# A two-layer decoder step on one core: how the low parts of the second layer's weights are made

## The chip, the core and the metric

The kernel runs on one core of a Trainium2 chip. A core has five engines that run side by side and wait for each other by semaphores: TensorE (PE: matrix products, with PEld, its weight loads), VectorE (DVE), ScalarE (ACT), GpSimd (POOL), and SyncE (SP), which here only issues transfers. Sixteen DMA engines move data between the large memory (HBM), on-chip memory (SBUF), and within SBUF. Products land in PSUM, which DVE and ACT read. The metric is the device time of one execution in microseconds (us); lower is better. The kernel before took 1169.92 us, the median of three runs (1169.79 to 1174.06).

## What is computed

One inference step of a two-layer trunk, for a prompt of 512 tokens and 8 samples of 8 tokens (576 columns in all), width 1024, in float32. Layer one is a gated linear recurrence; then one shared key/value projection; layer two is sliding-window attention with queries and gates of its own:

```python
for layer in range(DEPTH):
    if layer < N_A_LAYERS:
        hp, sp = hgrn2_layer(hp, s_zero, w_in_a[layer], w_out_a[layer], norm_a[layer], onorm_a[layer], lb[layer])
        ...
        kv_p = shared_kv(hp, norm_kv, w_kv)
        kv_s = shared_kv(hs, norm_kv, w_kv)
    else:
        q, gate = swa_in(hp, w_in_b[j], norm_b[j])
        hp = swa_out(hp, swa_prompt(q, kv_p, sinks_b[j]), gate, w_out_b[j])
        q, gate = swa_in(hs, w_in_b[j], norm_b[j])
        hs = swa_out(hs, swa_sample(q, kv_s, cache_kv_window, sinks_b[j]), gate, w_out_b[j])
```

`swa_in` is an RMS norm and a product with `w_in_b` (1024 x 4096: queries and gates); `swa_out` multiplies the attention output by silu(gate) and by `w_out_b` (2048 x 1024) and adds the input.

## The kernel before

**Split products.** A product of float32 data is made of three products in a faster format: activations and weights are each split into a high part, rounded to that format, and a low part, the rest. PE adds high x high, high weight x low activation, and low weight x high activation. `product_cols` (L207) orders them so: eight matmuls (one for each 128 rows) with the high weights `whi` and the high activations, eight with `whi` and the low activations, and last eight with the low weights `wlo`. A weight tile is used for two halves of the columns, 48 matmuls in all.

**Weight tiles.** `split_weights` (L195) makes one tile of 128 x 1024. SP loads 512 KB from HBM into `raw` (three buffers in rotation); ACT casts it to `whi` (L200); `wlo` is raw minus high (L204). `whi` and `wlo` have two buffers each, so a cast for a tile waits until PE has finished with the tile before the last. A number called the share says how many eighths of the subtraction DVE does; POOL does the rest. It is 8 in layer one, 2 for the key/value weights, and `LO_B` = 0 in the second layer (L1406): there POOL makes every low part.

**The second layer's tiles.** 16 tiles of query weights (`bq`), 16 of gate weights (`bg`) and 16 of output weights (`o`). Fourteen of the last kind use `whi_o` and `wlo_o`; the two tiles of the closing product (`out_last`, L477) use the memory of the activations' own parts `xhi` and `xlo`, which are no longer needed by then. All splits go through `split_weights`.

**Order.** The attention of the second layer and the products with weight tiles are woven by a list written by hand (`ORDER`, `merged`), so that PE has products to do while scores, exponentials and turns of the attention run on DVE, ACT and POOL. A scheduler then lays out the instructions for each engine in order of priority; each engine works through its list strictly in that order and waits at the first instruction that is not ready. POOL's list in this layer holds the subtractions, half of the scalings of the probabilities P (L1136), the last step of the gates (`silu`, L1343, after three ACT passes over `lb`, L1340 to L1342) and copies of V (`Vd`, L1356).

**Names in the rows.** At the start of the layer, `u_norm_b`, `xhi`, `xlo` are the normalized activations (`scaled`, L515), `kf` (L1030) the scaled key/value products, and `pvw` (L1062) turns of `kf` on PE. `pbq`, `pbg`, `po`, `pz` are the products with query, gate, output and closing tiles. `QS` (L1286, L1289) and `Qs` (L1294) are the queries, high and low parts; `ohb`, `olb` (L1394, L1395, L1266, L1267) the two parts of the gated attention output; `hT` (L1334) the residual stream; `Ps`, `oS`, `sts` belong to the samples' attention; `P`, `ph`, `pk`, `low` to the prompt's.

The closing lines of the split:

```python
act.copy(hi[:, :n], raw[:, :n])
c = n * share[0] // 8
for eng, r in ((dve, slice(0, c)), (pool, slice(c, n))):
    if r.start < r.stop:
        eng.tensor_tensor(lo[:, r], raw[:, r], hi[:, r].bitcast(F32), ALU.subtract)
```

## Time and profile before

| | |
|---|---|
| time, median of three runs | 1169.92 us |
| the profiled execution, its own time | 1169.39 us |
| its span, first to last instruction | 1167.6 us |
| TensorE clock granted, mean of the span | 0.982 of full speed |
| DMA packets' share of the 16 engines, main queue | 28.0% |
| HBM read / written | 84.06 MB / 14.16 MB |

A row of the timeline gives the start and the duration in us, then engine, line, operation, what it writes and reads (output<-inputs, by the program's names), the shape, and how many like it were merged; in brackets stands the engine's idle time before it and what ended that. A row of the waits gives who waited for whom, the total in us, how often, and the longest. A row of groups gives the busy time in us and the mean in ns, then the idle time before and who ended it. A row that begins with two times and a colon is a stretch of the span: its length, then the busy time of PE, PE's weight loads, DVE, ACT and POOL with their instructions, the granted clock, the DMA share, and GB/s. Busy times of PE are modelled for pipelined matmuls, so a busy PE need not be at its peak.

### The profile page before, as it was taken

Reading aid. Unit: us, or ns where it says so; the run is one execution under the profiler, and the core shown is the slowest. Engines: PE = TensorE matmul, PEld = TensorE weight load, DVE = VectorE, ACT = ScalarE, POOL = GpSimd, SP = SyncE. Lnnn points to the kernel's source line nnn. Section 1 sums busy time; section 2 is a strip of 40 time slices with the busy share of each in tenths; the row PEclk is TensorE's granted clock in tenths of the full one; section 3 lists DMA queues with packets and bytes.
Section 4 is the critical chain, followed back from the end, with each engine's and each line's share of the span. In section 5 each row is a group of like instructions: output and inputs, shape, how many; then the busy total and the mean of one; then the engine's idle time right before and its main releaser. Section 6 shows DMA issues by size and latency. Waiting matters only on the chain.

```text
span 1167.6 us, 27339 instructions
## 1 busy us (share of the span) xinstructions
PE 1111.7 (95%) x10937; PEld 1078.1 (92%) x10937; DVE 895.4 (77%) x2090; ACT 702.1 (60%) x1700; POOL 340.7 (29%) x311
## 2 busy tenths in 40 slices
PE   5999999999999999999999987999999999999997
PEld 5999999999999999999999987989989999999986
DVE  8898776489984597893897779567787778777686
ACT  6776764466662567772767455557655764765545
POOL 1122221112121131110122155444543453454430
PEclk8999999999999999999999998989999999999999
DMA  5332233232332523332232332211212213112102
GB/s 154 100 112 86 84 109 112 59 110 76 110 117 66 147 74 113 97 107 74 76 111 77 103 91 74 68 55 56 73 39 71 74 55 91 56 55 73 56 19 82
DMA packets 161097, 98.01 MB, mean 84 GB/s; under 512 B 3897, under 2 KB 157546, under 8 KB 160938
## 3 DMA queue, kind: packets, MB, share of 16 engines
q1 hardware_dynamic: 160970, 96.26, 28.0%
q8 instruction: 86, 1.41, 0.5%
q14 instruction: 41, 0.34, 0.1%
HBM read 84.06 MB, written 14.16 MB: 84 GB/s over the span
## 4 chain that ended last, share of the span: by engine, by line
PE 45%; DVE 11%; ACT 6%; issue 2%; POOL 1%; DVEq 0%; ACTq 0%; POOLq 0%
PE pbg L211 7%; PE po L211 7%; PE pbq L211 5%; PE po L228 4%; PE pg L228 3%; PE pf L228 3%; PE pi L228 3%; PE pq L228 2%; PE pkv L211 2%; PE sc L1098 2%; ACT P L1127 1%; PE pav L1181 1%; PE pz L211 1%; DVE QS L1289 1%; PE pa L797 1%
## 5 line engine op out<-in xcount | busy, mean ns | idle before, releaser
L606 POOL TENSOR_TENSOR Xl<-Xl 128x72 f32<-128x72 f32 x80 | 50.3, 659 | 205.9 <-DVE Xl L603 204.7
L638 POOL TENSOR_TENSOR sg<-sg,lg 128x576 f32<-128x576 f32 x16 | 26.3, 1642 | 278.4 <-ACT lg L571 278.4
L200 ACT CAST whi_a<-raw_a 128x1024 fp32r<-128x1024 f32 x64 | 67.1, 1049 | 63.4 <-PE po L228 30.8
L204 DVE TENSOR_TENSOR wlo_a<-raw_a,whi_a 128x1024 fp32r<-128x1024 f32 x64 | 81.8, 1282 | 25.0 <-issue 23.6
L1127 ACT ACTIVATE P<-P,st 128x192 f32<-128x192 f32 (+2 forms) x128 | 54.1, 424 | 68.4 <-DVE st L1122 68.4
L1136 POOL TENSOR_SCALAR P<-P,st 128x192 f32<-128x192 f32 (+1 forms) x64 | 48.6, 769 | 117.9 <-DVE st L1129 99.4
L438 DVE TENSOR_TENSOR hT<-hT,po 128x576 f32<-128x576 f32 x32 | 24.1, 754 | 49.6 <-PE po L228 49.3
L200 ACT CAST whi_o<-raw_o 128x1024 fp32r<-128x1024 f32 x30 | 31.4, 1047 | 30.8 <-PE po L228 25.6
L204 POOL TENSOR_TENSOR wlo_bg<-raw_bg,whi_bg 128x1024 fp32r<-128x1024 f32 x16 | 38.4, 2402 | 35.5 <-ACT whi_bg L200 30.0
L228 PE MATMUL po<-oh,whi_o 128*128 128x288 f32 x256 | 42.8, 302 | 4.4 <-ACT whi_o L200 1.9
L211 PE MATMUL po<-olb,whi_o 128*128 128x288 f32 x224 | 43.0, 306 | 3.8 <-DVE olb L1395 1.9
L211 PE MATMUL po<-ohb,whi_o 128*128 128x288 f32 x224 | 43.6, 311 | 2.4 <-DVE Qs L1294 1.7
L662 POOL TENSOR_TENSOR vb<-vst,bmask 128x512 fp32r<-128x512 f32 x32 | 36.7, 1168 | 26.7 <-DVE vst L658 13.8
L204 POOL TENSOR_TENSOR wlo_bq<-raw_bq,whi_bq 128x1024 fp32r<-128x1024 f32 x16 | 38.8, 2430 | 19.2 <-ACT whi_bq L200 19.1
L228 PEld LDWEIGHTS po<-oh,whi_o 128*128 128x128 f32 x256 | 35.9, 188 | 6.3 <-ACT whi_o L200 2.2
L211 PE MATMUL pbq<-xhi,whi_bq 128*128 128x256 f32 (+1 forms) x256 | 41.4, 305 | 0.0
L211 PE MATMUL po<-ohb,wlo_o 128*128 128x288 f32 x224 | 41.3, 301 | 0.0
L228 PE MATMUL po<-ol,whi_o 128*128 128x288 f32 x256 | 40.5, 294 | 0.0
L211 PE MATMUL pbg<-xhi,whi_bg 128*128 128x288 f32 x256 | 40.5, 300 | 0.0
L228 PE MATMUL po<-oh,wlo_o 128*128 128x288 f32 x256 | 40.4, 294 | 0.0
L211 PE MATMUL pbg<-xhi,wlo_bg 128*128 128x288 f32 x256 | 40.1, 299 | 0.0
L204 POOL TENSOR_TENSOR wlo_o<-raw_o,whi_o 128x1024 fp32r<-128x1024 f32 x14 | 33.6, 2399 | 22.0 <-ACT whi_o L200 20.3
(385 smaller groups left out, 3761.4 us busy)
## 6 DMA issues: line engine op xcount, KB each, us to landing
raw_a<-in_w_in_a_dram SPq DMA_DIRECT2D x64, 512.0 KB
S<-in_state_hgrn_dram SPq DMA_DIRECT2D x32, 256.0 KB
out_dram<-S SPq DMA_DIRECT2D x32, 256.0 KB
raw_o<-in_w_out_a_dram SPq DMA_DIRECT2D x16, 512.0 KB
raw_bq<-in_w_in_b_dram SPq DMA_DIRECT2D x16, 512.0 KB
raw_bg<-in_w_in_b_dram SPq DMA_DIRECT2D x16, 512.0 KB
raw_o<-in_w_out_b_dram SPq DMA_DIRECT2D x16, 512.0 KB
xt<-in_x_prompt_dram SPq DMA_DIRECT2D x4, 512.0 KB
```

The source lines that it names most:

```text
L200: act.copy(hi[:, :n], raw[:, :n])
L204: eng.tensor_tensor(lo[:, r], raw[:, r], hi[:, r].bitcast(F32), ALU.subtract)
L211: pe.matmul(pm[:, : c1 - c0], w[:, k * width + w0 : k * width + w0 + P], x(k)[i][:, c0:c1], start=n == 0, stop=n == len(terms) - 1,)
L228: pe.matmul(pm[:, j, :HN], w[:, k * width + c0 : k * width + c0 + P], x(k, j), start=n == 0 and k == 0, stop=n == 2 and k == nk - 1,)
L438: dve.tensor_add(h2, h2, ps2(pm))
L606: pool.tensor_tensor(X8[:, :, j : j + 1], X8[:, :, j : j + 1], X8[:, :, k : k + 1], ALU.add)
L638: (pool if SGP else dve).tensor_tensor(sg, sg, l, ALU.mult)
L662: pool.tensor_tensor(t, view(vst.bitcast(F32), [[0, 4], [1, P]], off=half * P), view(bmask, [[1, 4], [0, P]]), ALU.mult,)
L797: pe.matmul(pa[32 * j : 32 * j + ns, c, t0 : t0 + nt], keys[:, c * P + s0 : c * P + s0 + ns], queries[:, c * P + t0 : c * P + t0 + nt], st ...
L1098: pe.matmul(sc[:, hf, k0[hf] :], QS[pr][:, 2 * n + hf, :], kk[:, g, ks], start=q == 0, stop=q == 1)
L1127: act.activation(x, x, AF.Exp, bias=st[:, a : a + 1], accum_out=st[:, 8 + a : 9 + a])
L1136: (pool if e == "p" else dve).tensor_scalar(x, x, st[:, 8 + a : 9 + a], None, ALU.mult)
```

## The change

In the second layer the low part is no longer a subtraction on POOL. ACT makes the high part as before; a second ACT instruction writes the negated high part into `wlo`; then a transfer that is issued from POOL's list, with addition, adds the raw tile to what stands in `wlo`, inside SBUF. The other splits (share 8 and share 2) are as they were.

```diff
-LO_B = 0
+LO_B = None
...
         hi, lo = parts or [wts.tile([P, 1024], F32R, tag=t, name=f"{t}_{name}") for t in ("whi", "wlo")]
+        if share[0] is None:
+            act.copy(hi[:, :n], raw[:, :n])
+            act.activation(lo[:, :n], hi[:, :n].bitcast(F32), AF.Copy, scale=-1.0)
+            pool.dma_start(lo[:, :n].bitcast(F32), raw[:, :n], accum_op=ALU.add)
+            return hi, lo
         act.copy(hi[:, :n], raw[:, :n])
```

The lines below L200 move down by five in the changed file. The instructions do not only change in kind; the scheduler also places some of them elsewhere. POOL's list at the start of the second layer, before:

```order
L521 TENSOR_TENSOR xlo<-u_norm_b_0_9540,xhi 128x288
L204 TENSOR_TENSOR wlo_bq_9715<-raw_bq_9712,whi_bq_9714 128x1024
L204 TENSOR_TENSOR wlo_bq_9781<-raw_bq_9778,whi_bq_9780 128x1024
L521 TENSOR_TENSOR xlo<-u_norm_b_1_9600,xhi 128x288
L521 TENSOR_TENSOR xlo<-u_norm_b_1_9608,xhi 128x288
L521 TENSOR_TENSOR xlo<-u_norm_b_1_9616,xhi 128x288
L521 TENSOR_TENSOR xlo<-u_norm_b_1_9624,xhi 128x288
L1356 CAST Vd_9704<-Vc 64x512 x4
```

The same place in POOL's list with the change:

```order
L526 TENSOR_TENSOR xlo<-u_norm_b_0_9540,xhi 128x288
L203 DMA wlo_bq_9715<-raw_bq_9712 128x1024
L526 TENSOR_TENSOR xlo<-u_norm_b_1_9600,xhi 128x288
L526 TENSOR_TENSOR xlo<-u_norm_b_1_9608,xhi 128x288
L526 TENSOR_TENSOR xlo<-u_norm_b_1_9616,xhi 128x288
L526 TENSOR_TENSOR xlo<-u_norm_b_1_9624,xhi 128x288
L203 DMA wlo_bq_9782<-raw_bq_9779 128x1024
L1361 CAST Vd_9704<-Vc 64x512 x4
```

Two subtractions in a row gave way to two transfers, the second of which stands behind all low parts of the normalized activations. ACT's list around the last query tile and the gate tile after it, before:

```order
L1341 ACTIVATE lb_13887<-lb_13887 128x512
L200 CAST whi_bq_14031<-raw_bq_14029 128x1024
L1342 ACTIVATE lb_13887<-lb_13887 128x512
L1286 CAST QS_0_13905<-pbq_0_13913 64x4x64 x2
L1127 ACTIVATE P_0_2_13942,st_0_2_13943<-P_0_2_13942,st_0_2_13943 128x192
L1124 ACTIVATE st_0_2_13943<-st_0_2_13943 128x4
L1127 ACTIVATE P_0_2_13942,st_0_2_13943<-P_0_2_13942,st_0_2_13943 128x192 x3
```

The same place in ACT's list with the change:

```order
L1347 ACTIVATE lb_13923<-lb_13923 128x512
L1291 CAST QS_0_13941<-pbq_0_13950 64x4x64 x2
L202 ACTIVATE wlo_bq_14069<-whi_bq_14068 128x1024
L1132 ACTIVATE P_0_2_13979,st_0_2_13980<-P_0_2_13979,st_0_2_13980 128x192
L1129 ACTIVATE st_0_2_13980<-st_0_2_13980 128x4
L1132 ACTIVATE P_0_2_13979,st_0_2_13980<-P_0_2_13979,st_0_2_13980 128x192 x3
L201 CAST whi_bg_14178<-raw_bg_14176 128x1024
L1291 CAST QS_0_13941<-pbq_1_13995 64x4x64 x2
L1189 COPY low_0_0_14043<-pav_0_0_14039 64x512
L1161 CAST ph_0_1_14057<-ptr_0_1_14049 128x512
L1166 CAST pk_0_1_14061<-ptm_0_1_14050 64x256 x2
L202 ACTIVATE wlo_bg_14179<-whi_bg_14178 128x1024
```

The negation of the query tile stands behind the last pass over `lb` and behind two casts of queries; that of the gate tile stands six instructions behind its own cast. POOL's list at the same tile, before:

```order
L1356 CAST Vd_13855<-Vc 64x512 x4
L1136 TENSOR_SCALAR P_0_1_13769<-P_0_1_13769,st_0_1_13770 128x192 x2
L204 TENSOR_TENSOR wlo_bq_14032<-raw_bq_14029,whi_bq_14031 128x1024
L1343 TENSOR_TENSOR sgt_13661<-sgt_13661,lb_13887 128x512
L1136 TENSOR_SCALAR P_0_2_13942<-P_0_2_13942,st_0_2_13943 128x192 x2
```

and with the change:

```order
L1361 CAST Vd_13891<-Vc 64x512 x4
L1141 TENSOR_SCALAR P_0_1_13804<-P_0_1_13804,st_0_1_13805 128x192 x2
L1348 TENSOR_TENSOR sgt_13695<-sgt_13695,lb_13923 128x512
L203 DMA wlo_bq_14069<-raw_bq_14066 128x1024
L1141 TENSOR_SCALAR P_0_2_13979<-P_0_2_13979,st_0_2_13980 128x192 x2
```

The gate's last step (`sgt`), which came after the subtraction, now stands ahead of the transfer.

## The prediction

> **What bounds the kernel now.** I read the page's totals first, then TensorE's waits in the second layer (700 us to the end), then the timeline at each long wait.

> ```profile
> span 1167.6 us, 27339 instructions
> PE 1111.7 (95%) x10937; PEld 1078.1 (92%) x10937; DVE 895.4 (77%) x2090; ACT 702.1 (60%) x1700; POOL 340.7 (29%) x311
> ...
> 700.00:1168.00 468.00, 439.38 (x3409) 427.87 (x3407) 351.31 (x1064) 275.93 (x767) 205.59 (x154) 0.97 0.21 62
> ...
> PE pvw L1062 <- DVE kf L1030: 6.3, 1, 6.3
> PE scs L1205 <- DVE Qs L1294: 5.0, 2, 2.8
> PE po L211 <- DVE olb L1395: 1.9, 3, 1.6
> PE po L211 <- DVE olb L1267: 1.8, 1, 1.8
> PE po L211 <- DVE Qs L1294: 1.7, 1, 1.7
> PE pts L1223 <- DVE Ps L1217: 1.5, 1, 1.5
> PE po L211 <- DVE hT L1334: 0.5, 1, 0.5
> ```

> TensorE (PE) is busy for 95% of the span and for 439 of the last 468 us, so PE sets the time, and a change pays or costs only where PE waits. In the layer that the change touches PE waits some 19 us (the sum of the rows above), and each of them names VectorE (DVE). None names a low part: all are ready in time now. So there are two questions. Which of these DVE waits does GpSimd (POOL) cause, whose subtractions go? And are the low parts still in time when a transfer makes them?

> **What goes.** POOL's subtractions, in groups:

> ```profile
> L204 POOL TENSOR_TENSOR wlo_bq<-raw_bq,whi_bq 128x1024 fp32r<-128x1024 f32 x16 | 38.8, 2430 | 19.2 <-ACT whi_bq L200 19.1
> L204 POOL TENSOR_TENSOR wlo_bg<-raw_bg,whi_bg 128x1024 fp32r<-128x1024 f32 x16 | 38.4, 2402 | 35.5 <-ACT whi_bg L200 30.0 <-PE pbq L211 5.5
> L204 POOL TENSOR_TENSOR wlo_o<-raw_o,whi_o 128x1024 fp32r<-128x1024 f32 x14 | 33.6, 2399 | 22.0 <-ACT whi_o L200 20.3 <-PE pbq L211 1.7
> L204 POOL TENSOR_TENSOR xlo<-raw_o,xhi 128x1024 fp32r<-128x1024 f32 x2 | 4.8, 2392 | 5.2 <-ACT xhi L200 5.2
> L519 DVE SCALAR_TENSOR_TENSOR u_norm_b<-hT,vT,rall x12: 498/506/2618, 713.3 to 727.4; 128x288 f32<-128x288 f32 x12
> L1267 DVE TENSOR_TENSOR olb<-oS,ohb x16: 205/218/2430, 821.2 to 1141.1; 128x64 fp32r<-128x64 f32 x16
> ```

> These are 48 subtractions of 2.4 us, 115 us of an engine that nobody waits for. But the last two rows (shortest/median/longest, ns) show their price: a DVE instruction of 0.21 us once took 2.43, one of 0.50 took 2.62. Each time the excess is one POOL subtraction, as the timeline shows at the layer's start:

> ```profile
> 713.28 0.51 DVE L519 SCALAR_TENSOR_TENSOR u_norm_b<-hT,vT,rall 128x288 f32<-128x288 f32 x1
> ...
> 716.30 6.12 DVE L519 SCALAR_TENSOR_TENSOR u_norm_b<-hT,vT,rall 128x288 f32<-128x288 f32 x3
> ...
> 717.13 4.98 POOL L204 TENSOR_TENSOR wlo_bq<-raw_bq,whi_bq 128x1024 fp32r<-128x1024 f32 x2
> ...
> 724.78 0.69 PE L1062 MATMUL pvw<-ident,kf 128*128 128x128 f32 x2 [6.33 <-DVE kf L1030]
> ...
> 726.40 2.06 PE L211 MATMUL pbq<-xhi,whi_bq 128*128 128x256 f32 x8
> ...
> 729.78 1.11 PE L211 MATMUL pbq<-xhi,wlo_bq 128*128 128x256 f32 x8
> ```

> Three DVE instructions worth 3 x 0.51 = 1.53 us take 6.12, because two subtractions (4.98 us) run on POOL. That holds up kf behind them, and PE stands still for 6.33 us. Without the subtractions kf comes 6.12 - 1.53 = **4.6 us earlier**, and 1.7 us of the stall stay. After the stall PE also ran slowly: eight matmuls took 2.06 us that three lines on took 1.11. With a stall of 1.7 us I count most of that loss of 1 us as saved: **0.7**. What is late next is the normalized second half that pbq's second product reads; it hangs on the same DVE queue, which moves forward with kf. ScalarE (ACT) now does two negations among the casts there, 2.1 us, but DVE, not ACT, was the slower of the two.

> The same further on:

> ```profile
> 852.19 2.35 POOL L204 TENSOR_TENSOR wlo_o<-raw_o,whi_o 128x1024 fp32r<-128x1024 f32 x1 [0.72 <-ACT whi_o L200]
> 852.29 2.33 DVE L1267 TENSOR_TENSOR olb<-oS,ohb 128x64 fp32r<-128x64 f32 x1
> ...
> 854.67 0.40 PE L211 MATMUL po<-olb,whi_o 128*128 128x288 f32 x1 [1.83 <-DVE olb L1267]
> ...
> 1112.32 2.46 DVE L1256 TENSOR_TENSOR oS<-oS,sgS 128x256 f32<-128x256 f32 x1
> ...
> 1119.25 2.36 POOL L204 TENSOR_TENSOR wlo_o<-raw_o,whi_o 128x1024 fp32r<-128x1024 f32 x1 [1.75 <-ACT whi_o L200]
> ...
> 1119.73 3.04 DVE L1395 TENSOR_TENSOR olb<-sgt,ohb 128x512 fp32r<-128x512 f32 x2 [0.66 <-ACT ohb L1394]
> ...
> 1122.22 0.40 PE L211 MATMUL po<-olb,whi_o 128*128 128x288 f32 x1 [1.55 <-DVE olb L1395]
> ```

> At 852 an instruction of 0.2 us waits out a whole subtraction, and PE loses 1.83; at 1120 it loses 1.55. Both go: **3.4 us**. The 0.5 us behind hT (L1334, in the list of waits) follow the DVE row of 2.46 us at 1112, which is long beside a subtraction too; I count **0.5**. The waits for Qs (6.7 us in three) and Ps (1.5) are chains through ACT and DVE that hold no subtraction; they stay. Gains: 4.6 + 0.7 + 3.4 + 0.5 = **9.2 us**.

> **What is added on ACT.** 48 negations of 128x1024; the nearest row is the cast of the same shape.

> ```profile
> 787.01 1.05 ACT L200 CAST whi_bq<-raw_bq 128x1024 fp32r<-128x1024 f32 x1 [0.65 <-issue]
> ```

> 48 x 1.05 = 50 us on an engine that is busy for 276 of these 468 us; it goes to 326, or 70%. Its idle time covers it nearly everywhere. At two of the waits for Qs a negation now stands ahead of the casts that feed Qs. With no gain to bound it from below (an extra instruction excludes one) it costs 0 to 2.1 us; I take **1**. A negation also waits until PE has read the buffer's previous low part, one third of a product after the high part came free; the cast's own 1.05 us cover this.

> **What is added on the queues.** The low part is now ready when the transfer lands, not when POOL is done. No row shows an adding transfer inside SBUF. The nearest is the load of the same 512 KB from HBM:

> ```profile
> 1110.21 0.37 SPq L198 DMA_DIRECT2D raw_o<-in_w_out_b_dram  x1
> ...
> 1113.98 1.05 ACT L200 CAST xhi<-raw_o 128x1024 fp32r<-128x1024 f32 x1 [0.83 <-DMA raw_o<-in_w_out_b_dram]
> ...
> 1110.20:1111.20 1.00, 1.00 (x10) 1.00 (x10) 0.93 (x5) 0.95 (x3) 0.61 (x1) 1.00 0.00 0
> 1111.20:1112.20 1.00, 1.00 (x10) 1.00 (x9) 0.99 (x3) 0.96 (x3) 1.00 (x3) 1.00 0.39 133
> 1113.20:1114.00 0.80, 0.80 (x9) 0.80 (x8) 0.80 (x1) 0.02 (x1) 0.80 (x1) 1.00 0.10 38
> ```

> From issue to use 3.8 us: 1 us without traffic (the last column is GB/s), some 2.1 us of data, 0.7 until the waiting cast starts. An addition must also read what it adds to. If that costs nothing, 3.8 us; if the data phase doubles, 5.9; if everything doubles, 7.6. I take **5.0**, nearer the plain row than the doubled one, since there is no HBM on either side.

> [...]

> How much room is there? For each of the 46 tiles wlo_bq, wlo_bg and wlo_o I took the end of the work that now stands ahead of the transfer, plus 1.05, to PE's first matmul with the low part. Two tight tiles and a loose one:

> ```profile
> 1049.46 0.73 ACT L1286 CAST QS<-pbq 64x256 fp32r<-64x256 f32 x2
> ...
> 1055.91 1.12 PE L211 MATMUL pbq<-xhi,wlo_bq 128*128 128x256 f32 x8
> ...
> 1057.62 0.74 ACT L1161 CAST pk<-ptm 64x256 fp32r<-64x256 f32 x2
> ...
> 1064.10 1.22 PE L211 MATMUL pbg<-xhi,wlo_bg 128*128 128x288 f32 x8
> ...
> 799.87 1.12 PE L211 MATMUL pbq<-xhi,wlo_bq 128*128 128x256 f32 x8
> ```

> First tile: the negation follows the QS casts (1050.19), ends at 1051.24, and PE needs the tile at 1055.91: 4.7 us. Second: 1058.36 + 1.05 to 1064.10, again 4.7. Third: the negation follows the cast of 787.01 directly, 789.11 to 799.87, 10.8 us. Over all: least 4.4, eight tiles under 6, the middle one 8.4. At 5.0 us three tiles come 0.3 to 0.6 late: **1.5 us**. At 3.8 none does; at 5.9 seven do, 7 us in sum; at 7.6 half do, about 25. DMA engines have room (21% busy in this layer; 48 x 512 KB more). A raw buffer comes free only at the landing, some 3.5 us later than now, but three of them rotate over 9 us a tile, so loads stay ahead. Behind the transfer on POOL stand the scalings of P and the gates; POOL's wait for the negation replaces 2.4 us of subtraction, so they are no later.

> **Sum.** 1169.4 (this execution, its span of 1167.6 and 1.8 around it; the median of the runs is 1169.9) - 9.2 + 1 + 1.5 = **1162.7 us**.

> **Rivals.**
> - *The transfers are too late.* Landing in 6.5 to 7.6 us instead of 5: 12 to 25 us of waits for low parts, less the 8.2 net gain of the other terms: **1173 to 1186**, slower. It decides from about 6.1 us, where lateness eats the gain. For it: the addition's second read, and eight tiles under 6 us. Against: nothing in this layer keeps the DMA engines busy.
> - *POOL still holds DVE.* If writing the transfer's descriptors takes POOL about as long as a subtraction and blocks DVE likewise, the 9.2 us stay lost and ACT's 1 and the lateness come on top: **1170 to 1172**. [...] Against: no 512 KB pass through POOL any more. That is also the case in which the change does not do what it is written to do.
> [...]

> **Chances.** Forecast, landing in up to about 5.3 us, 1158 to 1164: 0.47. Descriptors held up, or landing near 5.9, 1164 to 1169: 0.20. POOL still holds DVE: 0.08. Transfers too late: 0.25, of which I keep up to 1182 in the range. At the low end, landing in 3.8 us, ACT at nothing and another 3 us of DVE delays gone: 1157. The range is 1157 to 1182. A measurement of this kernel can tell about 0.5%, 5.9 us: below 1164.1 is faster. Faster 0.47, within 0.28, slower 0.25.

> **What would show it.** Right: no wait of 6 us at pvw (under 2), no olb wait over 1 us, DVE's u_norm_b and olb rows with longest near their medians, and PE waiting for wlo in total under 3 us. Wrong: rows in which PE waits for a wlo transfer many times, 1 to 3 us each; or a POOL row of 2 us for the issue with DVE still stretched; or waits on QS and Qs that grew by a negation each.

## The result, and the profile after

| | before | after |
|---|---|---|
| median of four runs each | 1170.79 us | **1153.00 us** |
| range | 1169.79 to 1174.06 | 1150.15 to 1154.73 |
| the profiled execution, its own time | 1169.39 | 1152.44 |
| its span | 1167.6 | 1150.6 |
| clock granted, mean of the span | 0.982 | 0.987 |

The figures of before take in one run more than the three given at the start. The ratio is 0.9844, 95% interval 0.9828 to 0.9860: faster by 1.6%, 17.8 us between the medians. The forecast was 1162.7 and its range began at 1157: the direction was right, the size off by more than a factor of two.

The totals of the page of after, and below them from the windows the second layer from 700 us to the end of the span (the columns are those of the row shown before for 700 to 1168 us):

```profile
span 1150.6 us, 27472 instructions
PE 1105.9 (96%) x10937; PEld 1072.6 (93%) x10937; DVE 857.6 (75%) x2090; ACT 749.4 (65%) x1748; POOL 265.9 (23%) x311
```

```profile
700.00:1150.60 450.60, 433.14 (x3420) 421.71 (x3418) 313.40 (x1065) 323.03 (x815) 131.65 (x154) 0.99 0.51 120
```

The layer became 468.0 - 450.6 = 17.4 us shorter. Three columns tell how. DVE does the same work (1065 rows, 1064 before) in 313.4 us instead of 351.3: its rows are no longer stretched. PE stood idle for 450.6 - 433.1 = 17.5 us instead of 28.6: **11.2 us** less. And PE was busy for 433.1 us instead of 439.4 with the same matmuls: **6.2 us**, which no wait explains. The five longest waits of PE in the layer, after:

```profile
PE pbq L216 <- DMA wlo_bq<-raw_bq: 2.4, 2, 1.4
PE scs L1210 <- DVE Qs L1299: 2.1, 2, 1.1
PE po L216 <- DMA wlo_o<-raw_o: 2.1, 2, 1.7
PE pvw L1067 <- DVE kf L1035: 1.4, 1, 1.4
PE po L216 <- DVE olb L1400: 0.4, 2, 0.2
```

The wait for kf fell from 6.3 to 1.4 and those for olb from 3.7 to 0.4. But Qs fell too, from 6.7 to 2.1, and Ps is gone. New are four waits for a transfer, 4.5 us.

The rest was in the profile of before, in the column for the granted clock, when it is read in steps of a few us instead of over the whole layer. Before, in pairs of a stretch with a stall and what follows it:

```profile
719.30:722.70 3.40, 0.00 (x0) 0.00 (x0) 3.40 (x3) 0.62 (x2) 3.40 (x3) 1.00 0.46 129
722.70:729.60 6.90, 4.82 (x23) 4.75 (x24) 6.90 (x16) 3.17 (x8) 3.35 (x4) 0.51 0.34 92
773.90:777.30 3.40, 0.89 (x7) 0.66 (x6) 3.31 (x8) 1.27 (x3) 2.35 (x1) 1.00 0.53 154
777.30:784.20 6.90, 6.56 (x37) 6.02 (x38) 3.26 (x22) 1.87 (x10) 0.00 (x0) 0.51 0.27 78
852.40:855.80 3.40, 1.57 (x13) 1.33 (x12) 3.34 (x4) 0.00 (x0) 2.14 (x1) 1.00 0.02 6
855.80:859.30 3.50, 3.50 (x18) 3.50 (x17) 2.22 (x13) 1.56 (x8) 0.00 (x0) 0.51 0.50 144
958.20:961.60 3.40, 1.69 (x14) 1.55 (x14) 2.70 (x9) 3.08 (x7) 3.18 (x3) 1.00 0.01 2
961.60:965.10 3.50, 3.50 (x17) 3.50 (x16) 3.36 (x10) 0.00 (x0) 0.68 (x1) 0.51 0.47 146
```

Four times PE is idle for half of a stretch or more, and in what follows the granted clock is 0.50: 20.8 us in all, in which PE is busy for 4.82 + 6.56 + 3.50 + 3.50 = 18.4 us. Half of that, some 9 us, is an upper estimate of what the drops cost. After, up to the last products:

```profile
700.00:1140.00 440.00, 429.98 (x3397) 419.36 (x3396) 309.75 (x1058) 319.36 (x805) 131.65 (x154) 1.00 0.52 120
```

Not one drop is left. The new operations and two of the rows that were stretched before, by line (shortest/median/longest, ns; POOL's row is the issue alone):

```profile
L203 POOL DMA_DIRECT2D wlo_bq<-raw_bq x16: 857/896/1037, 720.4 to 1039.5; - x16
...
DMA to landing us min/median/max: 4.5/5.0/7.4
...
L524 DVE SCALAR_TENSOR_TENSOR u_norm_b<-hT,vT,rall x16: 504/508/1069, 697.2 to 725.5; 128x288 f32<-128x288 f32 x16
...
L1272 DVE TENSOR_TENSOR olb<-oS,ohb x16: 211/220/226, 813.3 to 1124.0; 128x64 fp32r<-128x64 f32 x16
```

A transfer lands 5.0 us after its issue in the median, as estimated. The longest olb row is 0.23 us instead of 2.43; the longest u_norm_b 1.07 instead of 2.62.

### The profile page after: what moved, and what is told of

It is laid out like the page before. It is cut to its first block, busy times and chain, and to the rows that moved or that the text cites. A ratio compares the mean times of both kernels' runs of the same rounds, so it can differ in the third digit from the quotient of the medians.

```text
span 1150.6 us, 27472 instructions
## 1 busy us (share of the span) xinstructions
PE 1105.9 (96%) x10937; PEld 1072.6 (93%) x10937; DVE 857.6 (75%) x2090; ACT 749.4 (65%) x1748; POOL 265.9 (23%) x311
## 4 chain that ended last, share of the span: by engine, by line
PE 51%; DVE 6%; ACT 3%; issue 1%; DMA 1%; POOL 0%; DVEq 0%; POOLq 0%; ACTq 0%
PE pbg L216 8%; PE pbq L216 8%; PE po L216 6%; PE po L233 4%; PE pg L233 3%; PE pf L233 3%; PE pi L233 3%; PE pq L233 2%; PE sc L1103 2%; PE pkv L216 2%; PE pav L1186 1%; PE pz L216 1%; PE pa L802 1%; PE ptr L1154 1%; DMA wlo_o<-raw_o 1%
## 5 line engine op out<-in xcount | busy, mean ns | idle before, releaser
L1132 ACT ACTIVATE P<-P,st 128x192 f32<-128x192 f32 (+2 forms) x128 | 54.1, 424 | 38.4 <-DVE st L1127 38.3
L216 PE MATMUL pbq<-xhi,wlo_bq 128*128 128x256 f32 (+1 forms) x256 | 39.9, 297 | 2.4 <-DMA wlo_bq<-raw_bq 2.4
L216 PE MATMUL pbq<-xlo,whi_bq 128*128 128x256 f32 (+1 forms) x256 | 39.3, 296 | 0.0
L233 PE MATMUL pf<-xhi,wlo_a 128*128 128x288 f32 x256 | 37.5, 299 | 1.8 <-DVE wlo_a L209 1.8
L233 PE MATMUL pf<-xhi,whi_a 128*128 128x288 f32 x256 | 39.1, 303 | 0.0
```

The lines of the kernel that those rows point to most:

```text
L216: pe.matmul(pm[:, : c1 - c0], w[:, k * width + w0 : k * width + w0 + P], x(k)[i][:, c0:c1], start=n == 0, stop=n == len(terms) - 1,)
L233: pe.matmul(pm[:, j, :HN], w[:, k * width + c0 : k * width + c0 + P], x(k, j), start=n == 0 and k == 0, stop=n == 2 and k == nk - 1,)
L1132: act.activation(x, x, AF.Exp, bias=st[:, a : a + 1], accum_out=st[:, 8 + a : 9 + a])
```

## The experiments

The kernel before ran beside each group of experiments, at medians of 1170.62 us (keep PE busy, negations alone, start on POOL, low parts on DVE), 1169.98 (POOL busy, negations earlier, the two that extend the change) and 1172.46 us (the last four); each ratio is to the runs beside it. Three theories stood against each other: (1) POOL's subtractions hold DVE up, and all that follows comes from there; (2) PE's clock drops behind stalls, and that is the half that the forecast missed; (3) the gain comes from where the scheduler put ACT's and DVE's instructions.

### Keep PE busy in the stalls of the kernel before

```diff
+    if c == 2 and n == 2:                     # ahead of the third turn of kf (pvw)
+        for _ in range(46): pe.transpose(pt[:, 3 * P :], ident, ident)
...
+    # inside two products, ahead of the waits for Qs (777 us, 18 of them) and olb (854 us, 11)
+    for _ in range(fill): pe.matmul(pm[:, : c1 - c0], zeros, x(0)[0][:, c0:c1], start=False, stop=False)
```

> The kernel before, with matmuls that PE can do while it waits at three of its stalls (46 turns of the identity before the third turn of kf, 18 products with a weight of zeros before the wait for Qs at 777 us, 11 before the wait for olb at 854 us), so that PE does not idle there; DVE, POOL and ACT do what they did, the low parts are still subtracted on POOL. Theory, the clock: in the profile of before the granted clock falls to 0.50 after these stalls (6.9 us, 6.9 us and 3.4 us of it), and that costs PE about 2.5 + 3.2 + 1.7 = 7.4 us; with PE kept busy the clock stays at 1.00 there, the waits themselves do not shrink, and the time falls by 4 to 8 us, to 1162 to 1166. The drop near 962 us, where nothing is filled, may stay. Rival, waits alone: the clock falls for another reason, or the lost speed is hidden behind DVE anyway: the time stays within 2 us of before, 1168 to 1172.

Measured: 1164.62 us, ratio 0.9943 (0.9929 to 0.9958), 6 us faster with 75 more matmuls. Its windows, at the same three places and at two later ones:

```profile
726.20:729.60 3.40, 3.37 (x28) 3.37 (x29) 3.14 (x9) 2.27 (x6) 2.40 (x2) 1.00 0.01 2
...
777.40:784.20 6.80, 6.80 (x57) 6.41 (x56) 4.86 (x28) 5.03 (x19) 1.62 (x3) 1.00 0.20 59
...
855.90:859.30 3.40, 3.40 (x29) 3.40 (x28) 3.27 (x7) 2.19 (x5) 3.34 (x3) 1.00 0.00 0
1060.70:1064.10 3.40, 1.34 (x14) 1.28 (x15) 2.70 (x8) 2.42 (x6) 3.40 (x3) 1.00 0.02 5
1064.10:1067.60 3.50, 3.50 (x17) 3.50 (x16) 2.62 (x8) 0.73 (x4) 0.01 (x1) 0.51 0.48 150
1115.40:1118.80 3.40, 1.64 (x11) 1.22 (x10) 3.40 (x8) 2.15 (x8) 1.42 (x1) 1.00 0.00 0
```

After 777 us PE gets through 57 matmuls in 6.8 us where it did 37 in 6.9. POOL still subtracts and DVE is still held (349.4 us busy in the layer, 351.3 before). So the drops cost time on their own, apart from the waits: theory 2 holds. The drop at 962 us, where nothing was filled, is gone too: its stall of 1.7 us now lies across an edge at 955.0 us between two stretches. Two new drops appeared, at 1064 and 1119 us, behind stalls that just escaped before. In sum some 20 us of drops became 7. In the two profiles PE's own products in the layer take 434.7 us instead of 439.4, while idle time and fillers together stay (28.1 us, 28.2 before): 4.7 of the 4.8 us between these two executions are products done faster.

### The negations alone

```diff
         act.copy(hi[:, :n], raw[:, :n])
+        if share[0] == 0:
+            act.activation(lo[:, :n], hi[:, :n].bitcast(F32), AF.Copy, scale=-1.0)
```

POOL's subtraction then writes over the negated part.

> The kernel before with ACT's 48 negations added (they write the low part's buffer, and POOL's subtraction then writes over them), without the adding transfers. This prices the negations alone. The forecast's term was 1 us with bounds 0 to 2.1: 1170 to 1172.5. Rival: on ACT they are on the path, 48 x 1.06 = 51 us of which a fifth shows: 1180. If the negations even help by their order, under 1169.

Measured: 1174.90 us, ratio 1.0034 (1.0023 to 1.0046): 4.3 us slower, outside the bounds of 0 to 2.1. This kernel tells more than was meant. PE's list is that of the changed kernel, row for row, and ACT's and DVE's are all but equal (5 of 1748 and 2 of 2090 rows stand elsewhere); what differs is that POOL subtracts instead of issuing a transfer. Its waits and its row for the layer:

```profile
PE scs L1207 <- DVE Qs L1296: 7.5, 2, 4.4
PE pvw L1064 <- DVE kf L1032: 3.1, 1, 3.1
PE sc L1100 <- DVE QS L1291: 2.3, 1, 2.3
```

```profile
700.00:1173.10 473.10, 443.76 (x3399) 431.46 (x3397) 353.09 (x1064) 323.38 (x815) 205.23 (x154) 0.96 0.21 61
```

With the changed kernel's order, Qs and QS are waited for longer than ever: 9.8 us, 7.4 before, 2.3 after. So it is not the order that freed them (against theory 3) but POOL. DVE needs 353.1 us for the 1064 rows that take 313.4 in the changed kernel, and the clock drops at six places instead of none. From here to the changed kernel lie some 22 us, between subtractions and transfers in the same order.

### POOL busy again

```diff
             pool.dma_start(lo[:, :n].bitcast(F32), raw[:, :n], accum_op=ALU.add)
+            for r in (slice(0, 512), slice(512, n)):
+                pool.tensor_tensor(spare[0], raw[:, r], hi[:, r].bitcast(F32), ALU.subtract)
```

> The changed kernel with POOL's subtractions added back as idle work (two of 512 columns for each tile, into a spare buffer that nobody reads; they stand ahead of the transfer in POOL's list, so the transfer is issued about 1.3 us later). The orders of PE, DVE and ACT are those of the changed kernel, one for one. Theory, POOL holds DVE: DVE's rows are stretched again by 30 us or more beside them, the waits for kf (5 to 6), Qs, Ps and olb come back, about 9 us in sum, and with them drops of the granted clock in three or more places, 5 to 9 us; the later transfers add some 5 to 8 us of waits for low parts: 1153 + 9 + 7 + 6 = 1175, range 1168 to 1182. Rival, the gain came from where the scheduler put ACT's and DVE's instructions: only the waits for low parts grow, the clock stays, 1157 to 1162.

Measured: 1173.92 us, ratio 1.0030 (1.0015 to 1.0046). The whole gain is gone, although the transfers make every low part. Waits, and the windows behind two of them:

```profile
PE pvw L1070 <- DVE kf L1038: 8.0, 1, 8.0
PE po L219 <- DVE hT L1342: 2.8, 2, 2.4
PE scs L1213 <- DVE Qs L1302: 2.6, 1, 2.6
PE pbq L219 <- DMA wlo_bq<-raw_bq: 2.3, 2, 2.0
PE po L219 <- DVE olb L1403: 2.0, 3, 1.3
PE po L219 <- DMA wlo_o<-raw_o: 2.0, 2, 1.1
PE po L219 <- DVE olb L1275: 1.1, 2, 0.8
```

```profile
721.80:725.20 3.40, 0.00 (x0) 0.00 (x0) 3.40 (x2) 0.73 (x2) 3.40 (x5) 1.00 0.50 96
725.20:732.10 6.90, 3.48 (x17) 3.44 (x18) 6.90 (x13) 2.73 (x7) 2.80 (x3) 0.51 0.43 108
```

The longest olb row was 1.34 us again, the length of one of the idle subtractions (1.29) and a little, where the changed kernel has 0.23. The waits for low parts did not grow (2.3 + 2.0 + 0.7 for one gate tile = 5.0, 4.5 after), though their transfers were issued later. The orders of PE, DVE and ACT are exactly the changed kernel's. This run and the one before it carry theory 1: what POOL works on makes the difference. Which wait it lengthens differs: here Qs and QS come to 3.6 us in sum and Ps is not waited for at all, against the expectation; kf, hT and olb take most.

### Only the start on POOL

```diff
-        if share[0] is None:
+        if share[0] is None and name not in ("bq0", "bq1"):
```

> The changed kernel, but the first two query tiles' low parts are subtracted on POOL again. Theory, wait and clock: the stall before the turns of kf comes back at about 6 us instead of 1.4 (+4.6), the clock falls to 0.50 for two stretches of 3.4 us behind it (+2.5), and two waits for transfers at the start go (-2): 1153 + 5 = 1158, range 1156 to 1161. Rival, waits alone: +4.6 - 2 = 1155.6 and no drop of the clock. Rival, the gain has nothing to do with the start: 1152 to 1154.

Measured: 1156.61 us, ratio 0.9868 (0.9853 to 0.9884): 3.6 us behind the changed kernel by the medians, 2.8 by the ratios.

```profile
PE pvw L1067 <- DVE kf L1035: 6.3, 1, 6.3
PE scs L1210 <- DVE Qs L1299: 2.1, 2, 1.1
PE po L216 <- DMA wlo_o<-raw_o: 2.0, 2, 1.8
PE pbq L216 <- DMA wlo_bq<-raw_bq: 1.0, 1, 1.0
```

```profile
719.60:723.00 3.40, 0.00 (x0) 0.00 (x0) 3.40 (x3) 0.49 (x2) 3.40 (x3) 1.00 0.48 127
723.00:730.00 7.00, 4.79 (x23) 4.73 (x24) 7.00 (x16) 3.30 (x8) 3.48 (x4) 0.51 0.32 92
```

The stall of 6.3 us and the 7 us at half clock are back; the later waits are the changed kernel's. By the rows it costs 4.9 more for kf, up to 2.4 for the clock (half of 4.79), and 1.4 less for wlo_bq: 5.9. Matched row by row with the changed kernel's profile, PE is 0.9 us ahead at 694 us and 3.6 behind at 733, so 4.5 us were lost at the start; the span grew by 3.2. The start's share of the gain is thus some 3 to 5 us.

### Low parts on DVE

```diff
-LO_B = 0
+LO_B = 8
```

> The kernel before, but DVE makes all low parts of layer two (share 8 instead of 0): no POOL subtractions and so nothing on POOL that holds DVE, no transfers, no negations, and 48 x 1.28 = 61 us more of DVE's own work. If holding DVE for 2.4 us at bad moments was what cost, then DVE is held for 1.28 us by its own subtraction, 48 times and not only where two meet: the waits for DVE stay in sum or grow, 1168 to 1176. [...]

Measured: 1165.68 us, ratio 0.9946 (0.9930 to 0.9962): 5 us faster than before and below the 1168 to 1176 expected.

```profile
PE scs L1205 <- DVE Qs L1294: 6.2, 2, 3.3
PE pvw L1062 <- DVE kf L1030: 2.8, 2, 1.8
```

```profile
700.00:1164.30 464.30, 440.37 (x3427) 428.25 (x3425) 368.04 (x1113) 276.73 (x767) 100.88 (x106) 0.98 0.21 63
```

DVE took on 48 subtractions of 1.22 us, 58.6 us, and is busy for only 16.7 us more (368.0 against 351.3): 42 us of the time before was being held. The kernel is 5 us faster although DVE is busy for longer. The waits for Qs stay, here behind DVE's own subtractions: two of them, of 1.21 and 1.23 us, stand between 767 and 776 us ahead of the first.

### Negations earlier

```diff
-            act.activation(...)
-            pool.dma_start(...)
+            with tc.high_priority(offset=800):
+                act.activation(...)
+                pool.dma_start(...)
```

> The changed kernel with a higher priority for the negation and the transfer, so that both stand earlier in ACT's and POOL's lists. This prices the late low parts (4.5 us of waits in the profile of the changed kernel). If the negation's place is what makes them late, the waits for low parts fall to 2 or less: 1149 to 1151. If the casts and the attention's passes behind it on ACT are what matters, they move back and DVE's and ACT's waits grow by as much: 1152 to 1157.

Measured: 1168.24 us, ratio 0.9981 (0.9964 to 0.9998): 15 us lost, far outside both expectations.

```profile
PE scs L1211 <- DVE Qs L1300: 3.6, 2, 3.3
PE pav L1187 <- DVE pk L1170: 2.2, 2, 1.3
PE pbg L217 <- DMA wlo_bg<-raw_bg: 1.9, 1, 1.9
```

The waits for low parts fell only to 3.4 us, the waits for the attention's steps grew by more (behind those shown, kcT 1.8 and ph 1.6), and three drops of the clock came back (775, 1065, 1120 us). DVE is not held here (312.7 us busy in the layer). So the order alone can cost as much as the change gains. It is not ACT's order alone: with the priority the scheduler also moved some 100 of DVE's rows, and the two were not taken apart.

### Other variants of the changed kernel

The key/value tiles by transfer as well, and then layer one too (the first line of the edit, and both):

```diff
-LO_KV = 2
+LO_KV = None
-LO_A = 8
+LO_A = None
```

> The changed kernel, and the four key/value tiles ahead of the second layer are made by negation and transfer too (they were subtracted, 2/8 on DVE and 6/8 on POOL). POOL's 4 x 1.9 us and DVE's 4 x 1.7 us near 681 to 708 us go. If POOL held DVE there as well, hT and kf come earlier: 1150 to 1152. If the transfers land too late there, 1154 to 1158.

> The changed kernel, and all weight tiles of layer one and the key/value product are made by negation and transfer too: DVE loses 80 subtractions of 1.22 us (98 us), ACT gains 80 negations of 1.06 us (85 us on an engine that is busy for 61% there). In layer one PE waits some 8 us for DVE in all, so the gain is at most about 8 us: 1145 if DVE was what it waited for and nothing lands late; 1155 to 1170 if low parts land late or ACT's waits grow.

Measured: 1156.74 us (0.9890, 0.9867 to 0.9912) and 1167.66 us (0.9978, 0.9960 to 0.9997). Neither beats the change alone. The first one's largest wait:

```profile
PE pkv L216 <- DMA wlo_kv<-raw_kv: 8.4, 3, 4.1
```

There is no room of 5 us ahead of these tiles. In the second, 5.1 us of the same wait stay, 4.7 for wlo_o come in layer one, and five drops of the clock stand between 300 and 701 us, where the changed kernel has two; the other causes there were not taken apart.

The changed kernel again, and three attempts to better it. The first raises the priority of one tile's negation and transfer (`o4_2`, the second output tile of the second group; no tile of this layer is called `o4_3`, so the edit is narrower than the expectation says):

> The changed kernel itself, beside the next three on the same chip: 1153, range 1150 to 1155, and a granted clock of 1.00 from 700 us to the last wait. Theory, a threshold: no stall of PE is long enough inside one stretch of 3.4 us. If the clock falls in single executions anyway, a drop of 3.4 us at 0.50 shows in the profile and costs 1.7 us or less.

```diff
+            with tc.high_priority(offset=100 if name in ['o4_2', 'o4_3'] else 0):
```

> The changed kernel, but for two of the eight output tiles of each of the first two groups and the first of the third (those of columns 256 to 512) the negation stands ahead of two ACT instructions that it stood behind; PE, DVE and POOL keep their order. In the profile of the changed kernel one of these tiles is the largest wait for a low part, 1.7 us. Theory: that wait goes to under 0.5 and nothing else changes, 1151.5 (1150 to 1153). Rival: the passes behind it are as urgent, 1153 to 1155.

The second splits each transfer:

```diff
-            pool.dma_start(lo[:, :n].bitcast(F32), raw[:, :n], accum_op=ALU.add)
+            for r in (slice(0, n // 2), slice(n // 2, n)):
+                pool.dma_start(lo[:, r].bitcast(F32), raw[:, r], accum_op=ALU.add)
```

> The changed kernel with each adding transfer split by columns into two of 256 KB, one behind the other in POOL's list. PE uses the columns in order, so it can start on the first half. Theory, lateness: the first half lands in about 4 us instead of 5, the second 0.9 later; the waits for low parts fall from 4.5 to 2 or less: 1150 to 1152. Rival: a transfer's time is mostly fixed and the first half lands no sooner; POOL has 48 x 0.9 us more to issue, and the last steps of the gates and the scalings of P come later: 1154 to 1158.

The third keeps PE busy in the wait at the kernel's start:

```diff
         pr = half(f"pr{i}")
+        if i == 3:
+            for _ in range(54): pe.transpose(pr[:, 256:384], ident, ident)
```

> The changed kernel with 54 turns of the identity for PE in the wait of 6.6 us before the first layer's first products (at 15.5 to 22.1 us), where the granted clock is 0.50 from 18.0 to 28.3 us in the profile of the changed kernel. Theory, the clock: PE loses about 3 us there at half speed; kept busy, it gains 1.5 to 3.5: 1150 to 1151.5. Rival: what follows waits for DVE and ACT anyway, or the scheduler's other order at the start costs as much: 1152 to 1155.

Measured, in this order: 1153.78 us (ratio 0.9837, 0.9822 to 0.9852); 1152.92 (0.9831, 0.9814 to 0.9848); 1157.48 (0.9864, 0.9844 to 0.9885); 1158.65 (0.9879, 0.9861 to 0.9896). The first confirms the result, again without a drop between 700 and 1140 us. The second can't be told from it: the wait for that tile is 1.3 us, 1.4 without the edit. Its transfer was issued 2.5 us sooner (at 947.62 instead of 950.11, in an execution that ran 1.1 us ahead), but landed after 6.1 us instead of 4.9, which took the lead away. Why it landed later is open, and so whether its place on ACT is what makes the tile late. The halves, in their profile:

```profile
L204 POOL DMA_DIRECT2D wlo_bq<-raw_bq x32: 845/966/1214, 720.8 to 1042.0; - x32
...
DMA to landing us min/median/max: 3.3/4.3/7.7
```

They land sooner and the waits for low parts fell to 2.9 us, but POOL now issues 96 times, mostly at about 1 us each, and two drops returned, behind longer waits for hT and kvs. The last kernel had its clock at 1.00 from 18 to 23 us, where the changed kernel's was 0.56 in the run beside it; but the fillers also made the scheduler place the first products in another order, and PE was busy for 29.7 of the 33 us from 27 to 60 instead of for all of them. The idea is not refuted, only this way to do it.

## Why the prediction was wrong

**Right: what POOL's subtractions held up directly.** Forecast 4.6 for kf, 3.4 for olb and 0.5 for hT, 8.5 us; the rows show 4.9 + 3.3 + 0.5 = 8.7. With POOL subtracting in the changed kernel's order these waits, 1.8 us in it, come back to 6.9 (negations alone) and 13.9 (POOL busy again).

**Mis-sized: the clock, 0.7 us in the sum, 6 to 9 in the runs.** This is the first of the two steps that failed. The forecast saw that eight matmuls behind the stall took 2.06 us instead of 1.11, counted that one loss, and let it rest there. The drop behind kf alone lasted 6.9 us, and there were three more, behind stalls of 2.8, 1.8 and 1.7 us. The mean clock of the layer, 0.97 in the row of windows that the prediction quotes, said it: 3% of 468 us is 14 us, part of it in PE's idle time. With PE kept busy in three stalls, and the other engines' lists as before but for six rows, the time fell by 6 us.

Only one of the four stretches of 3.4 us with these stalls, that at 719.3 us, was idle throughout; in the others PE was busy for 0.89, 1.57 and 1.69 us, and the clock fell to 0.50 behind them all the same.

**Wrong: "The waits for Qs (6.7 us in three) and Ps (1.5) are chains through ACT and DVE that hold no subtraction; they stay."** They went to 2.1 and nothing. This is the second step that failed. DVE works through one list, and a chain that itself holds no stretched row still starts late when rows before it were stretched. Two such rows, before:

```profile
754.20 1.33 DVE L1122 SCALAR_TENSOR_TENSOR st<-st,nsnk 128x4 f32<-128x4 f32 x1
...
950.27 2.39 DVE L1267 TENSOR_TENSOR olb<-oS,ohb 128x64 fp32r<-128x64 f32 x1
```

The first takes 0.16 us in the changed kernel and stands 23 us ahead of the wait for Qs at 777 us (2.8 us, 1.0 after); it makes the passes over P behind it 1.2 us late. What ran on POOL was `sgt`, right behind a subtraction. The second stands 11 us ahead of the wait at 961 us (1.7, none after). Two more such rows, of 1.52 and 1.21 us, stand at 1075 us, ahead of the wait for Ps. The run with negations and subtractions, in the changed kernel's order, has 9.8 us of waits for Qs and QS. Together with the smaller waits for QS and pl (1.2 to 0.2) that is about 7 us that the forecast put at nothing.

Not all of it is a gain. Ahead of the third wait for Qs, at 1068 us before (2.2 us, 1.1 after), no DVE row is stretched by more than 0.5 us in 40 us. There the changed kernel's PE has already waited, 11 us earlier, for a low part:

```profile
1044.56 0.62 PE L216 MATMUL pbq<-xhi,wlo_bq 128*128 128x256 f32 x3 [0.99 <-DMA wlo_bq<-raw_bq]
```

So some 1 us only moved from the waits for Qs to those for low parts.

**ACT's negations, +1 us.** In the changed kernel no wait of PE names a negation, though a part of the low parts' lateness is theirs. Added to the kernel before they cost 4.3 us, twice the upper bound, and with another order of ACT and DVE the changed kernel is 15 us slower. The term was small by grace of the scheduler's order, which the bounds didn't cover.

**Late low parts, 1.5 us; measured 4.5.** The landing time was right (5.0). What was wrong is the time at which PE needs the tiles: it was read from a timetable in which PE still stalled. The two largest waits, 1.7 and 1.4 us, are for tiles that PE reached before only behind a stall and a drop of the clock (Qs at 961, kf at 724). For the first, the forecast's way of counting gives 5.1 us of room in the profile of before (ACT's work ahead ends at 961.38, plus 1.05, to PE at 967.57); in the changed kernel it is 3.8 (949.99 to 953.75). A landing at 5.9, the data phase doubled, is refuted: it is above the median of 5.0 us and above the 4.5 to 4.6 of the transfers beside which nothing else moved.

**The rivals.** Transfers too late: no, 4.5 us of waits, not 12 to 25. POOL holds DVE while it issues: no; 0.90 us an issue, olb's longest row is 0.23, and the nine DVE rows that are still stretched by over 0.35 us stand beside other work of POOL. Descriptors held up, which stands in the line of chances: no run shows such a case; no issue of the changed kernel took longer than 1.04 us, and in the median a transfer landed 5.0 us after its issue began.

**The sum.** Waits: -8.7 - 7.1 + 4.5 and 0.3 for a small new one = -11.0; PE's idle time fell by 11.2. Clock: -6.2 by PE's busy time. Together -17.2; the layer became 17.4 us shorter, and the profiled executions differ by 17.0.

## What to carry to other kernels

A stall can have a second price: here the granted clock fell to 0.50 behind four stalls of PE, at a cost of 6 to 9 us. So look at the granted clock in steps of 3 us behind each stall, not at its mean (0.97 in this layer), and price a stall as its length plus what it slows behind it. When one engine's work is held up by another's, the delay need not end with the held instruction, since what stands behind it on that list starts late too (here the waits for Qs: 6.7 us before, 2.1 after), so a wait that names the held engine is suspect even where no long row stands in its own chain. A wait that shrinks may only have moved to another row, so add them all up. And read how much room a new, slower path has from the timetable that the change makes, not from the old one.

## What the runs showed of the hardware

**The adding transfers.** In the changed kernel 512 KB land in 5.0 us in the median and POOL spends 0.90 us on the issue. The eleven transfers of the changed kernel beside which no other packet moved landed in 4.5 to 4.6 us; six of the seven that took over 6.5 us had a whole load of 512 KB beside them. In the run with halves 256 KB land in 4.3 in the median, 3.3 at the least, with both halves of a tile under way together, so these runs do not tell which part of the time goes by size.

**POOL and DVE.** Beside a subtraction on POOL some of DVE's instructions with two inputs ended only when it had: olb's longest row is 2.43 us beside POOL rows of 2.4, 1.34 beside rows of 1.29, and 0.23 beside none. Before, in the second layer, 81 TENSOR_TENSOR and SCALAR_TENSOR_TENSOR rows and 120 others on DVE began beside a subtraction that had over 0.1 us more to run than such a row takes in the median. Of the 81, 25 were stretched, and ended 0.01 to 0.55 us after it; of the 120, none. What sets the 25 apart from the other 56 was not taken apart. A row stretched beside another product of two tiles on POOL is that at 754.20 (1.33 us, beside `sgt` of 1.31). Of the 45 us by which DVE's rows were stretched over the median of their like in this layer before, 36 stand beside subtractions, 5 beside `sgt`; after, 5 us are left in all.
